# A hybrid attention and mixture-of-experts layer: weight buffers on 512-byte boundaries, one transpose in another PSUM pool, and four additions in another order

## The chip, the cores and the metric

The kernel runs on one core of a Trainium2 chip, in float32. The metric is the device time of one execution in microseconds, the median of three runs. A profile is one more execution of the same program, with every instruction and every DMA packet recorded.

## What is computed

One layer of an encoder on 256 tokens of width 1024. The first half is a token mixer: a projection (`w_in`), differential attention beside a gated linear recurrence, two branch projections and an output projection. The second half, where nearly all the time goes, is a mixture of 32 experts of which each token uses 4:

```python
logits = xf @ router_w + router_b
top_v, top_i = lax.top_k(logits, 4)
gates = softmax(top_v)
# for each expert e, on the tokens xb that chose it:
gu = xb @ w_gate_up[e] + b_gate_up[e]      # 1024 -> 2048
g, u = split(gu, 2); g = min(g, 7); u = clip(u, -7, 7)
y = ((u + 1) * g * sigmoid(1.702 * g)) @ w_down[e] + b_down[e]   # 1024 -> 1024
out[token] += gate * y
```

Each expert has 8 MB of gate and up weights and 4 MB of down weights; all 32 are read once, 384 MB in all.

## The kernel before, in words

**Weight pieces.** Weights go through buffers of 8 KB per partition and 1 MB in all, called pieces. Pieces 0 to 15 lie in the pool `arena`, on the left of SBUF right behind the pool `const`; pieces 16 to 18 lie in the pool `mo`, on the right (L71, L861 to L863). The pieces are used in turn, 19 of them during the experts (`chunk` and `spot`, L85 to L92; the DMA is issued on L87, on SyncE's queue). A gate-and-up piece holds 128 rows of 8 KB, one per partition; a down piece holds two rows of 4 KB per partition. A piece can be loaded again when the last matmul that reads it is done.

**Where they start.** The left side begins with 16,512 bytes that the language reserves. Then come the tiles of `const`, among them `x` (8192 bytes per partition), `r2` (8 bytes, which take a slot of 32, L176), `acc` (8192) and `bgu` (4096). In the program that is built the arena starts at byte 40,480, which is 79 times 512 plus 32; as every piece is 8192 bytes long, all 16 start 32 bytes past a multiple of 512. The pool `mo` hangs from the right end; its pieces start at byte 190,432 and every 8192 on, 480 past a multiple of 512 (224 past one of 256). Its last tile is `w2` (4096 bytes, L1139).

**An expert.** The loop from L1131 takes the experts in order. Tokens are gathered for two experts at a time into `xg` (`gather`, L907; two gathers of two banks' worth stand in most experts behind the gate and up products, L1179). An expert takes one of three shapes by its number of tokens: up to 32 (`gate_up_32`, L948, `down_32`, L975), up to 64 (`gate_up_64`, `down_64`), and above 64, where the tokens from the 65th to the 96th are a first, extra pass: L1155 to L1159 for the products into `po`, and L1188 to L1190 for the rest. Call these three-step experts the heavy ones. Each choice is a branch that TensorE, VectorE and ScalarE take, and TensorE's order over the branches is written out by hand (`step`, `in_turn`).

The second half of an expert is, on TensorE, in this order: `transposed` (L958: the activation is turned in two banks, T1 in `psb` copied by ScalarE and T2 in `psc` copied by VectorE), `turned` (L992: the combination weights `gd` or `gdo` are turned, copied by ScalarE to `gt`), the down products (L972 or L980), and `combine` (L997: products of `gt` and `y` into four banks, two of `psc` and two of `psb`, then four additions to `acc` on VectorE, L1007). In a heavy expert this is done twice, first for the extra tokens with `so` and `gdo`, then for the first 64 with `act` and `gd`.

**PSUM.** There are three pools: `psa` with 4 banks, `psb` with 2, `psc` with 2 (L58 to L60). Each call of `bank` takes the next bank of its pool and waits until its last reader is done. Before, an expert takes three banks of `psa` (`pg`, `pu`, `po`, L1148). From `psc` it takes the gathers' banks, T2, the one of `turned` (L1020, `bank(psc)` where `pt` is None) and the first two of `combine`; from `psb` T1, the down products' bank `py`, and the last two of `combine`. The last expert has `pt` and `other` in `psa` (L1185), since its additions are left out and sums stay in PSUM.

Of the kernel before, what the change touches and what calls it, by code (L numbers as in the profile page):

```python
# [12 lines left out]
F32 = mybir.dt.float32  # L13
# [9 lines left out]
P = 128  # L23
D = 1024
S = 256
KD = D // P
NT = S // P
# [11 lines left out]
U = 32  # L39
# [10 lines left out]
def kernel(ctx, tc, a, out):  # L50
    nc = tc.nc

    const = ctx.enter_context(tc.tile_pool(name="const", bufs=1, side="left"))
# [4 lines left out]
    psa = ctx.enter_context(tc.tile_pool(name="psa", bufs=4, space=PSUM))  # L58
    psb = ctx.enter_context(tc.tile_pool(name="psb", bufs=2, space=PSUM))
    psc = ctx.enter_context(tc.tile_pool(name="psc", bufs=2, space=PSUM))  # L60

    def bank(pool, *shape):
        t = pool.tile([P, 512], F32, name="bank")
        if not shape:
            return t
        if len(shape) == 2:
            return t[:, : shape[0] * shape[1]].rearrange("p (a b) -> p a b", b=shape[1])
        return t[:, : shape[0]]
# [16 lines left out]
    def chunk(src, *shape):  # L85
        v = part(spot(), 0, *shape)
        nc.sync.dma_start(v, src)  # L87
        return v
# [5 lines left out]
    def part(t, off, *shape):  # L94
        t = ar(t) if isinstance(t, int) else t
        v = t[:, off : off + int(np.prod(shape))]
        if len(shape) == 2:
            return v.rearrange("p (a b) -> p a b", b=shape[1])
        if len(shape) == 3:
            return v.rearrange("p (a b c) -> p a b c", b=shape[1], c=shape[2])  # L100
        return v
# [71 lines left out]
    nc.gpsimd.iota(iota, pattern=[[1, S + CA]], base=1, channel_multiplier=0, allow_small_or_imprecise_dtypes=True)  # L173

    xn2 = part(11, 0, NT, D)
    r2 = const.tile([P, NT], F32, name="r2")  # L176
    acc = const.tile([P, NT, D], F32, name="acc")
    gw2 = const.tile([P, KD], F32, name="gw2")
    s2 = late.tile([P, D], F32, name="s2")
# [40 lines left out]
    pt = bank(psb, KD)  # L220
# [95 lines left out]
    pt = bank(psb, P)  # L316
# [544 lines left out]
    mo = ctx.enter_context(tc.tile_pool(name="mo", bufs=2, side="right", reuse_waits="tile"))  # L861
# [130 lines left out]
    def turned(gd, gt, pt):  # L992
        for t in range(NT):
            nc.tensor.transpose(pt[:, t * P : (t + 1) * P], gd[:, t], ident)  # L994
        nc.scalar.copy(gt, pt[:, :S])  # L995

    def combine(gt, y, n):  # L997

        pcs = [bank((psc, psb)[c // 2], NT, 256) for c in range(4)]
        order = range(4) if n == U else (0, 2, 1, 3)  # L1000
        for t in range(NT):
            for c in order:
                r, w = (U * c, 0) if n == U else (C * (c // 2), 256 * (c % 2))
                nc.tensor.matmul(pcs[c][:, t], gt[r : r + n, t * P : (t + 1) * P], y[r : r + n, w : w + 256], start=True, stop=True)  # L1004
        for c in order:
            cs = slice(256 * c, 256 * (c + 1))
            nc.vector.tensor_tensor(acc[:, :, cs], acc[:, :, cs], pcs[c], ALU.add)  # L1007

    def combine_into(fin, gt, y, n):

        for t in range(NT):
            for c in (range(4) if n == U else (0, 2, 1, 3)):
                r, w = (U * c, 0) if n == U else (C * (c // 2), 256 * (c % 2))
                nc.tensor.matmul(fin[c][:, t], gt[r : r + n, t * P : (t + 1) * P], y[r : r + n, w : w + 256],  # L1014
                                 start=False, stop=True, skip_group_check=True)

    def out_of(at, wd, n, y, gd, gt, fin, pt):

        py = bank(psb)
        turned(gd, gt, bank(psc) if pt is None else pt)  # L1020
        (down_64 if n == C else down_32)(at, wd, py)
        w = 512 if n == C else 256
        nc.scalar.copy(y[:, :w], py[:, :w])  # L1023
        combine(gt, y, n) if fin is None else combine_into(fin, gt, y, n)
# [47 lines left out]
    def rare(spare):  # L1072

        engines = [ET.PE, ET.Activation, ET.DVE, ET.SP]
        of = lambda i: nc.values_load(counts[0:1, i : i + 1], engines=engines, min_val=0, max_val=S)
        xr = mo.tile([P, KD, EB * CA], F32, name="xg")
        with tc.If(of(NE) > CA) as some:
            for e in range(NE):
                cnt = of(e)
                with tc.If(cnt > CA):  # L1080
                    rest_of(e, CA, xr, spare)
                    with tc.If(cnt > CA + P):
                        rest_of(e, CA + P, xr, spare)
        return some
# [17 lines left out]
    def load(e):  # L1102

        engines = [ET.PE, ET.Activation, ET.DVE]
        ins, (cnt,) = nc.values_load_multi_w_load_instructions(counts[0:1, e : e + 1], engines=engines, min_val=0, max_val=S,
                                                               skip_runtime_bounds_check_because="a sum of 256 zeros and ones")
        for i in ins:
            tc.keep_in_program_order(i)
        return cnt
# [3 lines left out]
    def step(ins):  # L1113

        if turns:
            tc.add_manual_dep(ins, turns[-1].name, NOSYNC, reason="order")
        turns.append(ins)
# [9 lines left out]

    down_loads = lambda e: [chunk(rows(a["w_down"][e], 2 * P * i, 2), 2, D) for i in range(4)]
    after = load(0)
    fin = pt = other = None  # L1130
    for e in range(NE):  # L1131
        j = e % EB
        cnt = after
        wg = [chunk(rows(a["w_gate_up"][e], P * k, 1), 1, 2 * DFF) for k in range(KD)]
        if e == NE - 1:
            wd = down_loads(e)
            step(rare(list(slots)[: len(slots) - KD - 4]).cond_inst)
        if e == LASTS:
            w2 = mo.tile([P, D], F32, name="w2", bufs=1)  # L1139
            for n, pr in enumerate(rows_of(gw2, psc)):  # L1140
                nc.scalar.copy(w2[:, 512 * n : 512 * (n + 1)], pr)
        if j == 0:
            xgn, todo = gather_batch(e + EB) if e + EB < NE else (None, [])
            fill = first if e == 0 else todo[:2]
        elif e < NE - 1:
            fill = todo[0 if e == 1 else 2 :] + (down_bias() if e == LASTS else [])
        xe = xg[:, :, j * CA : (j + 1) * CA]
        pg, pu, po = bank(psa), bank(psa), bank(psa)  # L1148
        act = mo.tile([P, 512], F32, name="s", bufs=1)
        so = mo.tile([P, 256], F32, name="so", bufs=1)  # L1150
        gd = mo.tile([P, NT, P], F32, name="gd", bufs=1)
        gdo = mo.tile([P, NT, P], F32, name="gdo", bufs=1)
        for ks in (range(4), range(4, KD)):
            last = ks[-1] == KD - 1
            with tc.If(cnt > C) as more:  # L1155
                gate_up_32(e, po, xe, wg, ks, C)
                if last:
                    swiglu(po[:, :256], po[:, 256:], so)
                    weights(e, gdo, C, U)  # L1159
            step(more.cond_inst)  # L1160
            with tc.If(cnt > U) as many:
                gate_up_64(e, pg, pu, xe, wg, ks)
                if last:
                    swiglu(pg, pu, act)
                    weights(e, gd, 0, C)
            with many.Else():
                gate_up_32(e, pg, xe, wg, ks, 0)
                if last:
                    swiglu(pg[:, :256], pg[:, 256:], act[:, :256])
                    weights(e, gd, 0, U)  # L1170
            step(many.cond_inst)
        if e == NE - 1:
            fin = [bank(pool, NT, 256) for pool in (psc, psc, psa, psa)]

            def begin(c):
                return nc.tensor.matmul(fin[c], ident, acc[:, :, 256 * c : 256 * (c + 1)], start=True, stop=False, skip_group_check=True)

            fill = [lambda c=c: begin(c) for c in range(4)]
        for g in fill:  # L1179
            in_turn(g)  # L1180
        if e < NE - 1:
            after = in_turn(lambda: load(e + 1))
            wd = down_loads(e)
        else:
            pt, other = bank(psa), bank(psa)  # L1185
        at = mo.tile([P, 4, P], F32, name="actT", bufs=1)
        y, gt = mo.tile([P, 512], F32, name="y", bufs=1), mo.tile([P, S], F32, name="gt", bufs=1)
        with tc.If(cnt > C) as more:  # L1188
            transposed(so, at[:, 0:2], 2, other)
            out_of(at[:, 0:2], wd, U, y, gdo, gt, fin, pt)  # L1190
        step(more.cond_inst)
        with tc.If(cnt > U) as many:
            transposed(act, at, 4, other)
            out_of(at, wd, C, y, gd, gt, fin, pt)
        with many.Else():
            transposed(act[:, :256], at[:, 0:2], 2, other)
            out_of(at[:, 0:2], wd, U, y, gd, gt, fin, pt)
        step(many.cond_inst)
        if j == EB - 1:
            xg = xgn  # L1200
# [72 lines left out]
```

## Time and profile before

| | us |
|---|---|
| median of 3 runs | 1243.11 (1241.19 to 1246.12) |
| the profiled execution, its own time | 1242.41 |
| its span | 1240.4 |
| TensorE busy in the span | 1009.2 (81%) |
| VectorE busy | 430.8 (35%) |
| ScalarE busy | 227.7 (18%) |
| DMA, mean over the span | 375 GB/s, 465.70 MB |

The span runs from the first to the last recorded instruction; 2.0 us of the profiled execution lie around it. The token mixer takes the first quarter, and the experts' weights flow from there to about 20 us before the end. TensorE's busy time counts matmuls from start to modelled end, so that a busy engine is not one at its peak.

### The profile page before, as it was taken

The page shows a single profiled execution, that of the slowest core. Times are in us where ns is not written, and L with a number is a line of the kernel's source. Part 1 is how long each engine was busy: PE and PEld are TensorE (multiplying, and loading weights), DVE is VectorE, ACT ScalarE, POOL GpSimd, SP SyncE. Part 2 cuts the span into 40 slices and gives each one's busy share as a digit, 9 for nine tenths or more (in the row PEclk, how much of TensorE's full clock was granted, in tenths as well). Part 3 has the DMA queues.
Part 4 walks back from the last instruction along what each step waited for, and adds up shares of the span by engine and source line. Part 5 has one row for each costly group of instructions (what it writes and reads, how often), then busy time and mean ns, then how long its engine had stood idle before and what let it go on. Part 6 is the DMA issues. An engine that isn't in the chain of part 4 may idle for free. (4 is left out here: it accounts for less than half of the span.)

```text
span 1240.4 us, 17345 instructions
## 1 busy us (share of the span) xinstructions
PE 1009.2 (81%) x6774; PEld 520.6 (42%) x6774; DVE 430.8 (35%) x843; ACT 227.7 (18%) x426; POOL 26.6 (2%) x36
## 2 busy tenths in 40 slices
PE   6999999998779899888799789668776667787845
PEld 3767777864433333433344333223332222333312
DVE  3498779642222222322222232212222212121212
ACT  3544656331111000100001110000100000010001
POOL 1020100010000000000000000000000000000000
PEclk9999989989999999999999999889989887888978
DMA  9967669879999999799999999999999999999994
GB/s 343 337 242 280 204 215 352 320 319 397 411 413 415 413 415 414 316 391 388 415 413 414 414 413 413 413 415 416 414 413 413 415 412 414 407 407 408 413 411 180
DMA packets 100191, 465.70 MB, mean 375 GB/s; under 512 B 9716, under 2 KB 9814, under 8 KB 67256
## 3 DMA queue, kind: packets, MB, share of 16 engines
q1 hardware_dynamic: 100024, 463.31, 93.7%
q8 instruction: 125, 2.05, 0.7%
q14 instruction: 42, 0.34, 0.1%
HBM read 462.23 MB, written 1.05 MB: 373 GB/s over the span
## 5 line engine op out<-in xcount | busy, mean ns | idle before, releaser
L955 PE MATMUL bank<-piece,xg 128*32 128x512 f32 x1472 | 209.7, 684 | 66.7 <-DMA piece<-in_w_gate_up_dram 54.8
L945 PE MATMUL bank<-piece,xg 128*64 128x512 f32 x768 | 170.7, 596 | 3.6 <-PEq L1155 2.7
L1007 DVE TENSOR_TENSOR acc<-acc,bank 128x512 f32<-128x512 f32 x136 | 84.4, 682 | 249.2 <-PE bank L1004 249.2
L923 DVE TENSOR_SCALAR bank<-bank 128x256 f32<-128x256 f32 (+1 forms) x35 | 18.3, 524 | 373.4 <-PE bank L955 260.4
L955 PEld LDWEIGHTS bank<-piece,xg 128*32 128x32 f32 x1472 | 43.8, 117 | 207.7 <-DMA piece<-in_w_gate_up_dram 123.8
L980 PE MATMUL bank<-piece,actT 128*32 128x256 f32 x1472 | 99.3, 421 | 6.0 <-DMA piece<-in_w_down_dram 2.7
L924 ACT ACTIVATE s<-bank 128x256 f32<-128x256 f32 (+1 forms) x32 | 14.8, 463 | 480.0 <-DVE bank L923 480.0
L945 PEld LDWEIGHTS bank<-piece,xg 128*64 128x64 f32 x768 | 56.1, 138 | 111.5 <-issue 100.5
L913 PEld LDWEIGHTS bank<-oh,x 128*128 128x128 f32 x512 | 87.7, 203 | 31.7 <-issue 22.0
L913 PE MATMUL bank<-oh,x 128*128 128x192 f32 (+1 forms) x512 | 96.8, 346 | 0.4 <-DVE xg L905 0.4
L972 PE MATMUL bank<-piece,actT 128*64 128x512 f32 x384 | 86.5, 604 | 0.8
L130 PE MATMUL bank<-lo,piece 128*128 128x512 f32 x208 | 84.1, 404 | 3.3 <-DVE lo L122 3.3
L131 PE MATMUL bank<-hi,piece 128*128 128x512 f32 x208 | 83.9, 403 | 0.0
L129 PE MATMUL bank<-hi,piece 128*128 128x512 f32 x208 | 82.6, 402 | 0.0
L122 DVE TENSOR_TENSOR lo<-piece,hi 128x1024 fp32r<-128x1024 f32 x60 | 74.0, 1254 | 16.7 <-ACT hi L121 16.5
L980 PEld LDWEIGHTS bank<-piece,actT 128*32 128x32 f32 x1472 | 49.3, 120 | 50.7 <-issue 18.3
L121 ACT CAST hi<-piece 128x1024 fp32r<-128x1024 f32 x60 | 62.0, 1047 | 45.0 <-PE bank L131 36.7
L964 PE MATMUL bank<-ident,s 128*128 128x128 f32 x88 | 17.0, 299 | 63.1 <-DVEq L1188 29.1
L1004 PE MATMUL bank<-y,gt 32*128 32x256 f32 (+1 forms) x544 | 49.2, 396 | 21.0 <-ACT y L1023 21.0
L1004 PEld LDWEIGHTS bank<-y,gt 32*128 32x128 f32 (+1 forms) x544 | 33.4, 185 | 44.2 <-ACT y L1023 42.1
L972 PEld LDWEIGHTS bank<-piece,actT 128*64 128x64 f32 x384 | 26.8, 139 | 52.8 <-issue 48.0
L1023 ACT COPY y<-bank 128x256 f32<-128x256 f32 (+1 forms) x35 | 15.6, 445 | 179.4 <-PE bank L980 96.9
(265 smaller groups left out, 875.2 us busy)
## 6 DMA issues: line engine op xcount, KB each, us to landing
piece<-in_w_gate_up_dram SPq DMA_DIRECT2D x256, 1024.0 KB, 20.2
piece<-in_w_down_dram SPq DMA_DIRECT2D x128, 1024.0 KB, 20.3
piece<-in_w_in_dram SPq DMA_DIRECT2D x22, 1024.0 KB, 6.6
piece<-in_w_mod_dram SPq DMA_DIRECT2D x16, 1024.0 KB, 8.3
piece<-in_w_mod_dram SPq DMA_DIRECT2D x16, 512.0 KB, 7.0
piece<-in_w_out_dram SPq DMA_DIRECT2D x4, 1024.0 KB, 5.1
piece<-in_w_branch_a_dram SPq DMA_DIRECT2D x2, 1024.0 KB, 8.0
piece<-in_w_branch_b_dram SPq DMA_DIRECT2D x2, 1024.0 KB, 7.5
```

The costliest lines, as they stand in the source:

```text
L121: now(A, lambda: nc.scalar.copy(hi, v[:, h]))
L122: now(V, lambda: nc.vector.tensor_tensor(lo, v[:, h], hi.bitcast(F32), ALU.subtract))
L129: nc.tensor.matmul(out, ah, bh, start=start, stop=False, skip_group_check=True)
L130: nc.tensor.matmul(out, ah, bl, start=False, stop=False, skip_group_check=True)
L131: return nc.tensor.matmul(out, al, bh, start=False, stop=stop, skip_group_check=True)
L913: last = nc.tensor.matmul(ph[:, j], x[:, t, k * P : (k + 1) * P], oh[:, t, cs], start=t == 0, stop=t == NT - 1)
L945: nc.tensor.matmul(pp[r : r + C], xg[:, k, :C], wg[k][:, 0, 512 * q : 512 * (q + 1)], start=False, stop=k == KD - 1, skip_group_check=True)
L955: nc.tensor.matmul(halves(po[U * q : U * q + U]), xg[:, k, s0 : s0 + U], quarter(wg[k][:, 0], q), start=False, stop=k == KD - 1, skip_grou ...
L972: nc.tensor.matmul(py[C * n : C * n + C], at[:, j, C * half : C * half + C], wd[kk // 2][:, kk % 2, 512 * n : 512 * (n + 1)], start=kk == ...
L980: nc.tensor.matmul(py[U * c : U * c + U, 0:256], at[:, j, U * q : U * q + U], wd[kk // 2][:, kk % 2, 256 * c : 256 * (c + 1)], start=kk == ...
L1004: nc.tensor.matmul(pcs[c][:, t], gt[r : r + n, t * P : (t + 1) * P], y[r : r + n, w : w + 256], start=True, stop=True)
L1007: nc.vector.tensor_tensor(acc[:, :, cs], acc[:, :, cs], pcs[c], ALU.add)
```

## The change

`r2` is given 512 bytes per partition instead of 8 and cut back to its two columns; `w2` is given 480 bytes more. The slot of `r2` grows from 32 to 512 bytes, so everything behind it on the left moves up by 480 bytes: the arena then starts at 40,960, 80 times 512. The pool `mo` grows by 480 and hangs from the right, so its pieces move down by 480, to 189,952, 371 times 512. The other tiles of `mo` move with them.

The bank of `turned` is taken from `psa` for every expert, once ahead of the branches, and serves both passes of a heavy one. An expert thus takes four banks of `psa`, which has four, and one fewer per pass of `psc`.

In `combine`, the passes over 32 tokens or fewer take the four banks in the order 2, 0, 3, 1 instead of 0, 1, 2, 3, in the products and in the additions. Banks 0 and 1 are of `psc`, 2 and 3 of `psb`.

```diff
@@ -173,7 +173,7 @@
-    r2 = const.tile([P, NT], F32, name="r2")
+    r2 = const.tile([P, P], F32, name="r2")[:, :NT]
@@ -997,7 +997,7 @@  def combine(gt, y, n):
         pcs = [bank((psc, psb)[c // 2], NT, 256) for c in range(4)]
-        order = range(4) if n == U else (0, 2, 1, 3)
+        order = (2, 0, 3, 1) if n == U else (0, 2, 1, 3)
@@ -1017,7 +1017,7 @@  def out_of(at, wd, n, y, gd, gt, fin, pt):
-        turned(gd, gt, bank(psc) if pt is None else pt)
+        turned(gd, gt, pt)
@@ -1127,7 +1127,7 @@
-    fin = pt = other = None
+    fin = other = None
@@ -1136,7 +1136,7 @@
         if e == LASTS:
-            w2 = mo.tile([P, D], F32, name="w2", bufs=1)
+            w2 = mo.tile([P, D + 120], F32, name="w2", bufs=1)[:, :D]
@@ -1182,7 +1182,8 @@
         else:
-            pt, other = bank(psa), bank(psa)
+            other = bank(psa)
+        pt = bank(psa)
```

## Rows read from the trace of the kernel before

**Rows 1.** The page: 40 equal slices of the span, 31 us each.

```profile
DMA  9967669879999999799999999999999999999994
GB/s 343 337 242 280 204 215 352 320 319 397 411 413 415 413 415 414 316 391 388 415 413 414 414 413 413 413 415 416 414 413 413 415 412 414 407 407 408 413 411 180
```

**Rows 2.** Windows: length, busy PE, PEld, DVE, ACT, POOL, clock, DMA share, GB/s.

```profile
440.00:460.00 20.00, 19.01 (x109) 7.64 (x106) 6.05 (x13) 2.16 (x5) 0.00 (x0) 1.00 1.02 419
...
480.00:500.00 20.00, 20.00 (x130) 6.08 (x124) 4.73 (x12) 0.38 (x1) 0.00 (x0) 1.00 1.01 412
500.00:520.00 20.00, 16.17 (x140) 8.57 (x138) 7.70 (x16) 3.26 (x8) 0.00 (x0) 1.00 0.70 279
...
580.00:1040.00 460.00, 356.19 (x2610) 149.37 (x2610) 113.37 (x251) 41.66 (x98) 0.00 (x0) 0.92 1.02 414
```

**Rows 3.** Waits of PE, 300 to 1222 us: total us, times, longest.

```profile
PE bank L955 <- DMA piece<-in_w_gate_up_dram: 54.8, 51, 2.2
PE bank L964 <- DVEq L1188: 28.0, 20, 1.9
...
PE bank L994 <- DVE xg L905: 3.3, 3, 1.2
```

**Rows 4.** The view of rows 2, three windows of 2 us where the transfers stop.

```profile
514.00:516.00 2.00, 1.93 (x13) 0.84 (x12) 0.47 (x2) 0.74 (x2) 0.00 (x0) 1.00 0.04 8
516.00:518.00 2.00, 2.00 (x12) 0.57 (x8) 0.00 (x0) 0.00 (x0) 0.00 (x0) 1.00 0.22 49
518.00:520.00 2.00, 2.00 (x12) 0.72 (x10) 0.00 (x0) 0.00 (x0) 0.00 (x0) 1.00 0.93 365
```

**Rows 5.** PE's timeline in two heavy experts: start, length, instructions, idle time before.

```profile
458.55 0.38 PE L964 MATMUL bank<-ident,so 128*128 128x128 f32 x2
459.92 0.41 PE L994 MATMUL bank<-ident,gdo 128*128 128x128 f32 x2 [0.99 <-DVE xg L905]
460.26 3.66 PE L980 MATMUL bank<-piece,actT 128*32 128x256 f32 x64
...
467.66 0.63 PE L964 MATMUL bank<-ident,s 128*128 128x128 f32 x4 [2.05 <-DVE acc L1007]
468.12 0.56 PE L994 MATMUL bank<-ident,gd 128*128 128x128 f32 x2
468.61 3.83 PE L972 MATMUL bank<-piece,actT 128*64 128x512 f32 x10
...
513.60 0.63 PE L964 MATMUL bank<-ident,s 128*128 128x128 f32 x4 [2.05 <-DVE acc L1007]
...
514.52 7.09 PE L972 MATMUL bank<-piece,actT 128*64 128x512 f32 x32
```

**Rows 6.** DVE's and ACT's timelines in the first of them, same columns.

```profile
459.29 0.48 DVE L905 TENSOR_SCALAR xg<-bank,sa,modc 128x192 f32<-128x192 f32 x1 [0.82 <-ACT xg L904]
459.69 0.28 DVE L965 COPY actT<-bank 128x128 f32<-128x128 f32 x1
465.63 2.48 DVE L1007 TENSOR_TENSOR acc<-acc,bank 128x512 f32<-128x512 f32 x4 [5.66 <-PE bank L1004]
468.32 0.42 DVE L965 COPY actT<-bank 128x256 f32<-128x256 f32 x1 [0.21 <-PE bank L964]
...
459.16 0.26 ACT L965 COPY actT<-bank 128x128 f32<-128x128 f32 x1
```

**Rows 7.** L994, all its matmuls on `gdo`: ns min/median/max, first and last start.

```profile
L994 PE MATMUL bank<-ident,gdo x6: 272/286/301, 459.9 to 861.3; 128*128 128x128 f32 x6
```

**Rows 8.** Windows as in rows 2: three `mo` pieces land; then sixteen `arena` pieces.

```profile
602.75:610.26 7.51, 6.25 (x36) 2.61 (x32) 0.92 (x2) 0.58 (x1) 0.00 (x0) 1.00 1.03 421
...
748.21:755.75 7.54, 7.22 (x36) 2.37 (x34) 0.03 (x1) 0.00 (x0) 0.00 (x0) 1.00 1.01 406
...
610.26:651.26 41.00, 33.50 (x243) 14.04 (x244) 10.93 (x25) 3.01 (x7) 0.00 (x0) 0.96 1.02 414
...
997.53:1038.45 40.92, 30.17 (x200) 12.19 (x196) 9.67 (x23) 3.81 (x9) 0.00 (x0) 0.75 1.02 413
```

## The prediction

> **What bounds the kernel now.** I read the slices first [rows 1]: from the ninth on the DMA engines are busy throughout and move 407 to 416 GB/s, except in slices 17 to 19 (316, 391, 388) and the last. The 384 MB of the experts, not an arithmetic engine, therefore set three quarters of the time: windows over the long undisturbed stretch give 414 GB/s at a DMA share of 1.02 [rows 2]. (The share passes 1 because the packets' recorded times overlap a little.) PE's waits say the same from the other side: it waits 54.8 us for gate and up pieces [rows 3]. So a change is worth something here in three ways only: if the transfers run faster, if they stop less often, or if the tail after the last piece is shorter.
>
> The transfers stop once for long, in the window of 500 to 520 us, which moves 279 GB/s instead of 414 [rows 2]: (1 - 279/414) x 20 = 6.5 us lost. The 2 us windows show the bottom at 514 to 518 us and the stream back at 518 [rows 4]. PE's timeline says why [rows 5]. Two heavy experts follow each other there, and between them PE is the late one: it is busy for all of the 20 us from 480 to 500 [rows 2]. The queue ran dry because the down pieces of the second heavy expert were still to be read; the first of them came free some matmuls into L972, which starts at 514.52, and the transfers came back 2 to 3 us later. There, and nowhere else in the experts, PE's chain is the path.
>
> **The change, part by part.** 1. *The bank of `turned`.* In the first pass of a heavy expert L994 waits for VectorE's gather (L905), because `turned` gets the `psc` bank that the second gather still holds: 0.99 us in the first heavy expert [rows 5], 3.3 us in three [rows 3]. With a bank of `psa` it can follow T2 at 458.55 + 0.38 = 458.93. But what comes next is late as well. L980 takes its first four matmuls from ScalarE's copy, ready at 459.16 + 0.26 = 459.42, and the others from VectorE's copy behind the same gather, ready at 459.69 + 0.28 = 459.97 [rows 6]. At 3.66/64 = 0.057 us each, 60 of them from 460.0 end at 463.45, against 460.26 + 3.66 = 463.92: 0.5 us are won, not 0.99. In the second heavy expert VectorE's copy is later in its queue, and I count 0.2. On the other experts' path there is nothing to win: L994 waits nowhere else, T1 and T2 before it do.
>
> 2. *The order of the additions.* T1 of the second pass waits 2.05 us [rows 5], since its `psb` bank is the one of the third addition; the four take 2.48 us from 465.63, 0.62 each [rows 6]. In the new order that bank is read first, so T1 can start at 465.63 + 0.62 + 0.15 = 466.4 instead of 467.66. Where T2 stands depends on part 1: with one `psc` bank fewer per pass its bank is that of the second addition, free at 467.0. Then `turned` (0.23 after T2's start, as the same four transposes take 0.46 now) and L972 at 467.8 instead of 468.6: 0.8 us. What is late next is VectorE's copy of T2, which stands behind all four additions in its queue and ends at 468.11 + 0.42 = 468.5. It is needed from L972's fifth matmul on, and four take 4 x 7.09/32 = 0.9 us, to 468.7: just covered. The new product order costs nothing by itself: the same 16 instructions with the same shapes in other banks. In light experts the next user of those banks comes behind all of the next expert's gate and up products, and nothing changes.
>
> So a heavy expert gains 0.8 + 0.2 to 0.5, about 1.1 us. Three are heavy, as L994 turns `gdo` six times, two transposes each, the last at 861 us [rows 7]. The first two both lie ahead of the stop, on PE's path, and bring the free pieces 2.2 us earlier; the third is covered by a full queue, whose stretch runs at 414 GB/s [rows 2]. The far ends: nothing, if the transfers that come back meet another late piece; 6.5 us, the whole stop.
>
> 3. *Four banks of `psa` out of four.* The next expert's `pg` no longer finds a bank that rested for a whole expert, but the one of this expert's `pg`. Its last readers are VectorE's steps of the activation, which come ahead of T1 of the same expert; the first product comes after `combine`. I take 0, with up to 2.48 us per expert (VectorE's additions, [rows 6]) as the far end on the slow side. No step is moved past a DMA queue or past POOL: the changes touch PE, ACT and DVE only, and SP's order is the same.
>
> 4. *The boundaries.* No piece of the kernel before starts on a multiple of 512, but the two kinds start differently: 32 bytes past one of 256 in the arena, 224 past one in `mo`. So the trace can say what the distance costs. Counted in bytes back from the end of the stream, three `mo` pieces land in a row every 19 MB. The nine such windows between 600 and 1000 us average 414.2 GB/s (406 to 421), and the nine of arena pieces behind them 413.9 (413 to 416) [rows 8]. The difference, 0.3, is within what nine windows with a scatter of 5 can say, 1.6 GB/s or 0.4%. I take 0. The rows cannot test a distance of zero. The far end for a gain is the best 20 us window, 419 GB/s [rows 2]: 937 us of stream (285 to 1222) x (1 - 414/419) = 11 us. For a loss it is the 0.4%, 4 us.
>
> The rows on the landing pieces are what speaks here. [...]
>
> The sum: against the profiled execution 1242.41 - 2.2 = 1240.2; that execution is 0.7 below the median, so the forecast is 1243.1 - 2.2 = 1240.9. A measurement of this kernel can tell about 0.5%, 6.2 us, from no change; the forecast lies within that.
>
> **Rivals.** *The boundaries pay.* Then the stream runs as in its best window, 1240.9 - 11 = 1230. For it: no row excludes a gain at distance zero, and the stream's rate sets the time. Against it: two kinds of distance, one rate [rows 8]. I give it 0.16. [...]
>
> *The spare bank is missed* (slower). The first product of an expert waits until VectorE is through its additions. For it: PE does wait 28.0 us in 20 places for VectorE to reach a branch [rows 3], although the banks concerned were long free, so a wait on an old reader can be put down to a later point. Then PE loses up to 31 x 2.48 = 77 us. 55 of them fall in time that it waits for weights anyway [rows 3], so that it decides from about 55/31 = 1.8 us per expert on; at the full price 1240.9 + 22 = 1263. Against it: the second product bank, `pu`, already follows `pg` of the expert before, and no wait of L945 for VectorE shows. 0.07.
>
> *VectorE takes it back.* The copies of T1 and T2 gate the down products, and the second heavy pass gains nothing because its copy stands behind the additions: then 1243. This is also the time if the order of banks comes out otherwise than I counted. 0.10.
>
> **How the numbers follow.** The forecast's own case has 0.67, with 1237 to 1245: the sum, less or plus the 4 us of part 4. Faster by over 0.5% (below 1236.9): most of the 0.16 and a little of the main case's edge, 0.17. Slower by over 0.5% (above 1249.3): 0.07. Within: 0.76. The range reaches to 1233 on the side of the boundaries, into that rival but not to its end, and to 1247 on the other, the loss of 4 us and the spread of runs; it leaves out the missed bank and the far part of the boundaries' gain.
>
> **What would show it.** Right: L994's wait for L905 gone; T1 of the second heavy pass waiting about 0.8 us instead of 2.05, L972 following within 1.5 us; the stop at 514 to 518 us shorter by about 2 us; the long stretch still at 414 GB/s. Wrong: 416 GB/s or more over 580 to 1040 us (the boundaries pay), or a wait of L935, L945 or L955 for VectorE at the start of an expert (the missed bank).

## The result, and the profile after

The changed kernel takes 1228.59 us (median of 4 runs, 1223.81 to 1229.64) against 1242.15 before: a ratio of 0.988, 95% interval [0.9842, 0.9917]. (A ratio and its interval are estimated from all runs of both kernels; it can differ by up to 0.2% from the ratio of the two medians.) The forecast was 1240.9 with a range from 1233 to 1247, so the time lies outside, on the fast side. What happened is the first rival: the boundaries pay. The profiled execution took 1229.55 us with a span of 1227.6.

The slices of the page after (40 slices, 30.7 us each) show it at a glance beside [rows 1]:

```profile
GB/s 348 359 234 274 202 188 349 310 330 369 415 421 423 422 423 423 317 399 379 424 421 423 422 422 422 422 423 423 424 422 420 423 421 420 417 413 421 422 413 174
```

Over the long stretch (slices 20 to 34), where 412 to 416 stood, 420 to 424 stands. The stop is still in slices 17 to 19. The windows of [rows 2] and [rows 4] for the kernel after (length, busy time of the engines, clock, DMA share, GB/s):

```profile
440.00:460.00 20.00, 20.00 (x113) 7.60 (x110) 4.95 (x11) 1.49 (x3) 0.00 (x0) 1.00 1.02 426
...
500.00:520.00 20.00, 17.76 (x140) 8.87 (x138) 7.30 (x16) 3.17 (x8) 0.00 (x0) 0.91 0.69 273
...
580.00:1040.00 460.00, 363.39 (x2718) 153.04 (x2718) 116.49 (x257) 42.54 (x100) 0.00 (x0) 0.92 1.02 422
...
514.00:516.00 2.00, 2.00 (x10) 0.74 (x8) 0.00 (x0) 0.00 (x0) 0.00 (x0) 0.74 0.00 0
516.00:518.00 2.00, 2.00 (x12) 0.62 (x10) 0.00 (x0) 0.00 (x0) 0.00 (x0) 1.00 0.65 172
```

The long stretch runs at 422 GB/s instead of 414, 1.9% more, at the same DMA share. The stop costs about as much as before (273 instead of 279 GB/s in its window).

The heavy experts on PE's timeline (start, length, instructions, idle time before), to be read beside [rows 5]:

```profile
460.50 0.38 PE L964 MATMUL bank<-ident,so 128*128 128x128 f32 x2
460.72 0.38 PE L994 MATMUL bank<-ident,gdo 128*128 128x128 f32 x2
461.43 3.78 PE L980 MATMUL bank<-piece,actT 128*32 128x256 f32 x64 [0.32 <-ACT actT L965]
465.76 1.15 PE L1004 MATMUL bank<-y,gt 32*128 32x256 f32 x16 [0.55 <-ACT y L1023]
467.75 0.41 PE L964 MATMUL bank<-ident,s 128*128 128x128 f32 x2 [0.85 <-DVE acc L1007]
468.35 0.41 PE L964 MATMUL bank<-ident,s 128*128 128x128 f32 x2 [0.19 <-DVE acc L1007]
468.60 0.38 PE L994 MATMUL bank<-ident,gd 128*128 128x128 f32 x2
468.91 7.09 PE L972 MATMUL bank<-piece,actT 128*64 128x512 f32 x32
...
512.24 8.45 PE L972 MATMUL bank<-piece,actT 128*64 128x512 f32 x32
...
557.54 0.62 PE L935 MATMUL bank<-bgu,sel 96*32 96x512 bf16 x4 [4.06 <-issue]
```

This part came as forecast: L994 follows T1 and T2 at once, T1 of the second pass waits 0.85 us instead of 2.05, T2 0.19 more, and L972 follows. From L964 on `so` to L972 the first heavy expert takes 468.91 - 460.50 = 8.41 us; before, 468.61 - 458.55 = 10.06 [rows 5].

Where the 14 us come from is read from two instructions that both kernels issue in the same order: the first product of the expert behind the stop (L935), and the first of the last sums (L1176). Before:

```profile
558.60 0.62 PE L935 MATMUL bank<-bgu,sel 96*32 96x512 bf16 x4 [4.14 <-issue]
...
1218.14 3.70 PE L1176 MATMUL bank<-acc,ident 128*128 128x512 f32 x8
```

After:

```profile
1204.01 3.70 PE L1176 MATMUL bank<-acc,ident 128*128 128x512 f32 x8
```

At L935 the kernel after is 1.1 us ahead (557.54), at L1176 14.1 us. Between them lie 660 us of stream, and 660 x (1 - 414/422) = 12.5 us is what the rate explains of the 13.1. Ahead of the stop the faster stream won nothing that lasts; the experiments come back to this.

### The profile page after: what moved, and what is told of

Read it like the earlier page. It is cut to its first block, busy times and chain, and to the rows that moved or that the text cites. A ratio compares the mean times of both kernels' runs of the same rounds, so it can differ in the third digit from the quotient of the medians.

```text
span 1227.6 us, 17342 instructions
## 1 busy us (share of the span) xinstructions
PE 1010.9 (82%) x6774; PEld 521.1 (42%) x6774; DVE 429.9 (35%) x843; ACT 227.6 (19%) x426; POOL 25.5 (2%) x36
## 3 DMA queue, kind: packets, MB, share of 16 engines
q8 instruction: 125, 2.05, 0.6%
## 5 line engine op out<-in xcount | busy, mean ns | idle before, releaser
L955 PE MATMUL bank<-piece,xg 128*32 128x512 f32 x1472 | 209.6, 688 | 58.3 <-DMA piece<-in_w_gate_up_dram 45.7
L945 PE MATMUL bank<-piece,xg 128*64 128x512 f32 x768 | 170.4, 594 | 4.8 <-PEq L1155 2.7
L955 PEld LDWEIGHTS bank<-piece,xg 128*32 128x32 f32 x1472 | 45.1, 118 | 201.9 <-DMA piece<-in_w_gate_up_dram 106.9
L945 PEld LDWEIGHTS bank<-piece,xg 128*64 128x64 f32 x768 | 55.5, 137 | 112.6 <-issue 100.6
L972 PE MATMUL bank<-piece,actT 128*64 128x512 f32 x384 | 86.4, 603 | 0.7
L964 PE MATMUL bank<-ident,s 128*128 128x128 f32 x88 | 17.2, 295 | 55.8 <-DVEq L1189 34.8
L972 PEld LDWEIGHTS bank<-piece,actT 128*64 128x64 f32 x384 | 26.9, 139 | 52.4 <-issue 49.1
```

The costliest lines, as they stand in the source:

```text
L945: nc.tensor.matmul(pp[r : r + C], xg[:, k, :C], wg[k][:, 0, 512 * q : 512 * (q + 1)], start=False, stop=k == KD - 1, skip_group_check=True)
L955: nc.tensor.matmul(halves(po[U * q : U * q + U]), xg[:, k, s0 : s0 + U], quarter(wg[k][:, 0], q), start=False, stop=k == KD - 1, skip_grou ...
L972: nc.tensor.matmul(py[C * n : C * n + C], at[:, j, C * half : C * half + C], wd[kk // 2][:, kk % 2, 512 * n : 512 * (n + 1)], start=kk == ...
```

## The experiments

The kernels ran in four groups, each beside the kernel before; its median in the four was 1243.67, 1245.02, 1244.95 and 1245.34 us. All ratios are to it.

**The two halves of the change.** The paddings alone, on the kernel before:

```diff
-    r2 = const.tile([P, NT], F32, name="r2")
+    r2 = const.tile([P, P], F32, name="r2")[:, :NT]
-            w2 = mo.tile([P, D], F32, name="w2", bufs=1)
+            w2 = mo.tile([P, D + 120], F32, name="w2", bufs=1)[:, :D]
```

> The two paddings alone; banks and order of the additions as before. Theory 1 (the boundaries made the stream faster): the long stretch runs at 422 GB/s as after the whole change, the two heavy experts keep their waits of 2.05 us, and the time is about 2 us above the changed kernel: 1230 to 1231 us, ratio about 0.990. Theory 2 (the shorter heavy experts made the gain and the rate follows from fewer stops): 414 GB/s and about 1240 to 1242 us.

Measured: 1232.26 us, ratio 0.9887 [0.9857, 0.9917], and the long stretch:

```profile
580.00:1040.00 460.00, 364.37 (x2722) 155.02 (x2714) 114.00 (x251) 42.87 (x101) 0.00 (x0) 0.91 1.02 422
```

The other half, the kernel after without the paddings (the diff above, undone):

> The bank of the combination weights and the order of the additions alone; pieces at 32 and 480 past a multiple of 512 as before. Theory 1: 414 GB/s in the long stretch, the waits in the heavy experts as in the changed kernel, and about 2 us less than before: 1240 us, ratio 0.998. Theory 2: 422 GB/s and about 1229 us, ratio 0.989.

Measured: 1239.63 us, ratio 0.9965 [0.9941, 0.9989].

```profile
580.00:1040.00 460.00, 359.47 (x2668) 152.02 (x2664) 111.12 (x246) 42.47 (x100) 0.00 (x0) 0.91 1.02 414
```

The rate goes with the paddings, whatever the heavy experts do: theory 2 falls. By the medians the paddings are worth 11.4 us and the banks with the order 4.0; by the intervals of the ratios, 10 to 18 us and 1.4 to 7.3. (The paddings move other tiles as well, `acc` among them; a run below, with half of the pieces off the boundary, moves pieces and the small tiles behind them alone, and the rate follows.)

**Which boundary.** The kernel after with other paddings, so that all 19 pieces start 64, 128 or 256 bytes past a multiple of 512 (the tile of `r2` has 16, 32 or 64 columns, and 120 of `w2` becomes 104, 88 or 56):

```diff
-    r2 = const.tile([P, P], F32, name="r2")[:, :NT]
+    r2 = const.tile([P, 64], F32, name="r2")[:, :NT]
-            w2 = mo.tile([P, D + 120], F32, name="w2", bufs=1)[:, :D]
+            w2 = mo.tile([P, D + 56], F32, name="w2", bufs=1)[:, :D]
```

> The changed kernel with all pieces 64 bytes past a multiple of 512. If a distance that is a multiple of 64 is enough, the stream runs at 422 GB/s and the time is that of the changed kernel, 1228 us. If it takes 256 or 512, the stream stays at 414 GB/s and the time is that of the banks alone, 1240 us; a value between would say that the cost grows with the distance.

Measured: 1236.5 us, ratio 0.9934 [0.9911, 0.9957].

```profile
580.00:1040.00 460.00, 360.52 (x2688) 152.30 (x2684) 113.34 (x249) 42.53 (x100) 0.00 (x0) 0.91 1.02 415
```

> The changed kernel with all pieces 128 bytes past a multiple of 512. At 256 the long stretch ran at 422 GB/s, at 64 at 415. Theory 1 (a transfer must start at a multiple of 256): 414 to 415 GB/s and 1236 to 1240 us. Rival (128 is enough): 422 GB/s and 1225 to 1229 us.

Measured: 1238.01 us, ratio 0.9943 [0.9919, 0.9966].

```profile
580.00:1040.00 460.00, 362.13 (x2672) 152.21 (x2668) 113.05 (x250) 42.45 (x100) 0.00 (x0) 0.91 1.02 415
```

> The changed kernel with all pieces 256 bytes past a multiple of 512. [...]

Measured: 1224.6 us, ratio 0.9837 [0.9805, 0.9869].

```profile
580.00:1040.00 460.00, 361.79 (x2716) 152.50 (x2716) 113.91 (x251) 42.47 (x100) 0.00 (x0) 0.93 1.02 422
```

At 256 the stream has its full 422 GB/s, at 128 and 64 it has 415, hardly more than at 32. Whether 256 is even better than 512, as 1224.6 against 1228.59 could suggest, was asked by the changed kernel once more:

> The changed kernel once more, beside the others: 1228 us by its four runs. With all pieces at 256 the time was 1224.6 us at the same 422 GB/s; if 512 and 256 are the same to the transfers, this run lies within 1224 to 1230 and its rate is 422.

Measured: 1224.53 us (1223.04 to 1229.51, 5 runs), ratio 0.9857 [0.983, 0.9884], 422 GB/s. So 256 and 512 are the same within the noise: the changed kernel's own medians differ by 4 us from one group of runs to the next.

**Does each piece pay for itself?** One padding without the other puts 3 or 16 of the 19 pieces off the boundary.

> The changed kernel with the padding of r2 alone: sixteen pieces on multiples of 512, the three on the right at 480 past one. If every piece pays for its own start, the long stretch runs at (16 x 422 + 3 x 414)/19 = 420.7 GB/s, the windows in which the three right pieces land at 414 and the others at 422, and the time is 1.9 us above the changed kernel's (3/19 of 11.8). If pieces that start off a boundary slow their neighbours in the queue too, the rate is nearer 414 and the windows don't differ.

Measured: 1227.1 us, ratio 0.9871 [0.9844, 0.9898].

```profile
580.00:1040.00 460.00, 360.67 (x2702) 150.12 (x2706) 113.85 (x251) 42.53 (x100) 0.00 (x0) 0.91 1.02 422
```

When each kind of piece passes can be counted: the 384 pieces of the experts stand in the order in which the program issues them, and their bytes are counted back from the end of the stream. By this count the windows of [rows 8] stand four pieces too late. The three `mo` pieces that the row 748.21:755.75 is said to hold pass at 737.0 to 744.5 us; and where they pass at 640.0 to 647.7, the last has landed by 650.1, before the window that was taken for them (651.26) begins. Placed by the count, over nine rounds, the three pieces at 480 land at 421.8 GB/s on average and the sixteen on the boundary at 421.3; in the changed kernel, with all on it, the same places have 421.6 and 422.4. Both theories fell: the three pieces don't pay the full price, nor do they slow the others.

> The changed kernel with the padding of w2 alone: the three pieces on the right on multiples of 512, the sixteen on the left at 32 past one. If every piece pays for its own start: 415.3 GB/s, the windows of the right pieces at 422, and 1237 to 1239 us. If one kind sets the pace of all: 422 or 414 in both kinds of window.

Measured: 1236.6 us, ratio 0.9933 [0.9899, 0.9968].

```profile
580.00:1040.00 460.00, 355.09 (x2684) 149.88 (x2680) 113.93 (x251) 42.46 (x100) 0.00 (x0) 0.93 1.02 416
```

Here the three pieces on the boundary land at 417.4 GB/s and the sixteen off it at 415.1, where paying for itself meant 422 and 414. In the kernel before the same places have 413.7 and 413.8. Windows of 7.5 us scatter by 5 GB/s and more, so the 417.4 is a rough figure.

With half of the pieces off the boundary, by 32 bytes more behind the eighth piece of the arena:

```diff
-    piece = lambda i, dt=F32: (arena if i < NA else mo).tile([P, 2048], dt, name="piece", tag=f"ar{i}", bufs=1)
+    piece = lambda i, dt=F32: (arena if i < NA else mo).tile([P, 2056 if i == 15 else 2048], dt, name="piece", tag=f"ar{i}", bufs=1)[:, :2048]
```

> The changed kernel with 8 of the 19 pieces 32 bytes past a multiple of 512 and 11 on one. With 19, 16, 3 and 0 pieces off the boundary the long stretch ran at 414, 416, 422 and 422 GB/s. If the loss goes as the share of pieces off the boundary, it is 8 x 8/19 = 3.4 and the rate 418.6. If it goes as the chance that two transfers off the boundary meet, the square of the share, it is 8 x 0.18 = 1.4 and the rate 420.6.

Measured: 1226.61 us, ratio 0.9854 [0.9816, 0.9892].

```profile
580.00:1040.00 460.00, 357.09 (x2696) 149.81 (x2692) 113.75 (x251) 42.54 (x100) 0.00 (x0) 0.93 1.02 420
```

| pieces off the boundary | measured, GB/s | if the loss goes as their share | as the square of it |
|---|---|---|---|
| 19 of 19 | 414 | 414 | 414 |
| 16 of 19 | 416 | 415.3 | 416.3 |
| 8 of 19 | 420 | 418.6 | 420.6 |
| 3 of 19 | 422 | 420.7 | 421.8 |
| 0 of 19 | 422 | 422 | 422 |

Neither law fits all three rates between the ends. With one more digit, from the packets' sizes and starts, these are 415.5, 419.7 and 421.7: the share is too low by 0.2, 1.1 and 1.0, the square too high by 0.8, 0.9 and 0.1. The five kernels with all pieces on the boundary and all experts' work lie within 0.3 of each other, so the loss does not add up piece by piece. The same padding of `w2` is worth 1.7 GB/s beside sixteen pieces off the boundary (413.8 to 415.5) and 0.3 beside sixteen on it (421.7 to 422.0).

In the run with half of them, six pieces off the boundary and then six on it stand in a row in each round. One round, and the same places in the changed kernel:

```profile
885.06:900.47 15.41, 13.75 (x155) 5.62 (x154) 3.81 (x8) 1.02 (x4) 0.00 (x0) 1.00 1.01 412
900.47:915.42 14.95, 10.34 (x98) 6.12 (x96) 3.39 (x10) 2.40 (x6) 0.00 (x0) 0.77 1.01 423
...
889.87:905.09 15.22, 13.62 (x152) 4.92 (x150) 3.37 (x7) 1.01 (x3) 0.00 (x0) 1.00 1.02 418
905.09:919.96 14.87, 10.56 (x96) 6.50 (x96) 3.82 (x11) 2.42 (x6) 0.00 (x0) 0.77 1.02 425
```

Over eleven rounds the six off the boundary land at 415.3 GB/s and the six on it at 421.5; in the changed kernel the same places have 420.3 and 421.7. So six in a row do pay, 5 GB/s of the 8. The packets' own durations say it with less scatter. A packet of 8 KB takes 313 ns (median) in the kernel before and 309 in the changed one. With half of the pieces off, it takes 313 in the middle of the six off the boundary and 309 in the middle of the six on it. But in the middle of three pieces it takes 309 both when they alone are on the boundary and when they alone are off it. So the price is not the transfer's own alone; it depends on what else passes around it. Six in a row at 32 bytes past paid and three at 480 did not; whether the number in a row or the distance makes that difference was not tried apart.

**Where the gain ahead of the stop went.** The kernel after without the extra pass of the heavy experts (their tokens from the 65th to the 96th are left out), with the pieces on and off the boundary; the condition is changed in both places where it stands:

```diff
-        with tc.If(cnt > C) as more:
+        with tc.If(cnt > S - 1) as more:
```

> The changed kernel without the extra pass of the three heavy experts (their tokens from the 65th to the 96th are left out). If the stop at 514 us gives back what the faster stream wins ahead of it, then without the stop the boundaries are worth the rate's difference over the whole stream, 937 x (1 - 414/422) = 17.8 us, between this kernel and the same one with the pieces off the boundary. If the gain ahead of 514 us is lost elsewhere, the difference stays at 11 to 14 us.

> The same kernel without the extra pass, with the banks and the order of the change, but the pieces at 32 and 480 past a multiple of 512 as before. Both theories: 414 GB/s. With the stop as the cause: 17 to 18 us above the kernel with the pieces on the boundary; otherwise 11 to 14.

Measured: 1216.2 us (0.9766 [0.9731, 0.9801]) on the boundary and 1235.65 (0.9912 [0.9884, 0.9941]) off it. The slices of the page, first on, then off:

```profile
GB/s 352 357 234 286 208 203 363 310 321 383 417 421 423 422 423 422 422 422 423 422 422 423 421 422 422 421 417 422 421 420 417 422 416 422 408 417 416 418 420 157
```

```profile
GB/s 340 341 242 284 193 197 345 320 324 391 400 413 414 414 414 414 414 414 415 413 414 415 414 414 413 413 408 416 408 415 408 413 410 408 408 404 412 411 409 169
```

The stop is gone in both, and the boundaries are now worth 19.5 us by the medians, a little more than the 17.8 expected, and not 11 to 14. Off the boundary the long stretch ran at 412 GB/s, not at the 414 expected, and on it at 420.

The intervals of these two times are wide, about 4 us either way each, but the profiles agree. From the first L994, at the start of the experts, to the first L1176 the two take 899.8 and 917.2 us, 17.4 apart. With the extra pass it is 909.2 and 907.9 on the boundary (the changed kernel's two profiles) and 921.0 off it (banks and order alone), 12 to 13 apart. And from the first L994 to L935 behind the stop these three take 262.7, 263.2 and 262.0 us: with the stop, nothing of the gain is left there. The reading is that PE sets when the transfers come back at 517 us, whatever the stream's rate was till then. The stop therefore takes back what the stream wins in its first 230 us.

**Bank and order apart.** The bank alone, on the kernel before (`order` as it was, the paddings undone):

> The bank of the combination weights in the products' pool alone; order of the additions and boundaries as before. L994's wait for the gather is gone and L980 waits for VectorE's copy in its place, 0.2 to 0.5 us won in a heavy expert; T1 of the second pass keeps its wait of 2.05 us. 1241 to 1243 us, and 414 GB/s. If instead the bank is the larger part of the 4 us that both won, about 1240.

Measured: 1245.37 us, ratio 1.0009 [0.9988, 1.003]. PE's timeline in the first heavy expert:

```profile
459.25 0.38 PE L994 MATMUL bank<-ident,gdo 128*128 128x128 f32 x2
459.95 3.78 PE L980 MATMUL bank<-piece,actT 128*32 128x256 f32 x64 [0.32 <-ACT actT L965]
...
467.47 1.09 PE L964 MATMUL bank<-ident,s 128*128 128x128 f32 x4 [2.04 <-DVE acc L1007]
...
468.92 9.43 PE L972 MATMUL bank<-piece,actT 128*64 128x512 f32 x32
```

The order alone, on the kernel before:

```diff
-        order = range(4) if n == U else (0, 2, 1, 3)
+        order = (2, 0, 3, 1) if n == U else (0, 2, 1, 3)
```

> The order of the additions alone; bank and boundaries as before. Theory 1 (the order does all that bank and order did together, as the wait of 2.04 us that it shortens also costs the clock of the products behind it): T1 of the second pass waits about 0.85 us, L972 in the first heavy expert takes 7.1 us at a granted clock of 1.00 instead of 8.6 at 0.91, and the time is that of both, 1240 us, ratio 0.9965. Rival (the two need each other, since the bank of T2 comes free only with the other pool): T2 waits longer, and 1242 to 1243 us.

Measured: 1243.84 us, ratio 0.9992 [0.9971, 1.0013].

```profile
473.73 0.41 PE L964 MATMUL bank<-ident,s 128*128 128x128 f32 x2 [0.85 <-DVE acc L1007]
474.32 0.41 PE L964 MATMUL bank<-ident,s 128*128 128x128 f32 x2 [0.19 <-DVE acc L1007]
475.52 0.66 PE L994 MATMUL bank<-ident,gd 128*128 128x128 f32 x2 [0.79 <-DVE acc L1007]
```

The waits bear the rival out: the two need each other. (The times agree, but 0.9965 for both, 1.0009 and 0.9992 for one alone, lie within each other's noise when added up.) With the order alone T1 comes early, and then `turned` waits 0.79 us, as its `psc` bank is that of the fourth addition: 0.85 + 0.19 + 0.79 = 1.83 us in place of 2.05. With the bank alone T1 keeps its wait. Only where `turned` has left `psc` does the early T1 reach L972. The last run says the same in the changed kernel:

> The changed kernel without the bank: both paddings and the order of the additions. If the bank of the combination weights is worth nothing, the time is that of the changed kernel, 1224 to 1229 us, and the long stretch runs at 422 GB/s. If it is worth 0.2 to 0.5 us in each heavy expert ahead of the stop, up to 1 us more than that.

Measured: 1230.62 us, ratio 0.9885 [0.9851, 0.992], the same as the paddings alone (0.9887), with the wait of 0.79 us back in each heavy expert. No version that was tried and computes the whole layer beats the changed kernel by more than the noise.

## Why the prediction was wrong

What bounds the kernel was read rightly: the stream sets the time behind the stop, PE ahead of it, and "if the transfers run faster" was the first of the three ways named.

The step that failed is part 4, "I take 0". It compared pieces 32 bytes past a boundary with pieces 224 past one, found 414 GB/s for both, and took the lack of a difference for the lack of a cost. All pieces were off a boundary, so the comparison had no case without the cost. Starts at 32 (with three pieces at 480), 64 and 128 bytes past a multiple of 512 give 414 to 415 GB/s, starts at 256 and 0 give 422: the term put at 0 is 8 GB/s, 2% of the rate, and 11.4 us. The sentence that the rows can't test a distance of zero stood in the text, yet the 4 us on either side, which became the main case's range, were taken from that comparison. They priced the scatter of a contrast that did not contain the case to be forecast.

The comparison was also misplaced: by the count above, its `mo` windows hold pieces of the arena. Placed right, it gives 413.7 and 413.8 GB/s, the same null. Even in the right place such short windows tell little: with the three `mo` pieces on the boundary and the sixteen others off it, they read 417.4 against 415.1. What 480 costs when all pieces are there, no run shows.

That the far end of 11 us met the 11.4 of the paddings is luck: the stream rose to 422 and not to 419, and the gain came from the 660 us behind the stop and not from 937. A gain at distance zero, which no row excluded, deserved the middle of the range, not 0.16.

Twice the distance did not cost more: 64 and 128 bytes past a multiple of 512 both give 415 GB/s. Why 256 is enough and 128 is not, no run shows.

Part 1 was right as a bound: what comes next is late as well, and the bank alone is worth nothing that could be measured. Part 2 was right in its waits (0.8 forecast, 0.85 measured) and in that T2's bank depends on part 1; that `turned` itself would wait for the fourth addition if it stayed in `psc` was not seen. The term may have been too small: 2.2 us forecast, 4.0 measured for bank and order together, with an interval of 1.4 to 7.3. In the first heavy expert 10.06 - 8.41 = 1.65 us were won instead of 1.1, and L972 behind it shows a further part, 7.09 us instead of 8.55. That instruction and the stretch of 460 to 480 us, before:

```profile
468.61 8.55 PE L972 MATMUL bank<-piece,actT 128*64 128x512 f32 x32
...
460.00:480.00 20.00, 16.66 (x140) 7.60 (x144) 3.40 (x6) 2.07 (x5) 0.00 (x0) 0.91 1.02 414
```

and with bank and order but without the paddings:

```profile
460.00:480.00 20.00, 17.67 (x162) 7.53 (x154) 5.81 (x11) 1.70 (x4) 0.00 (x0) 1.00 1.02 412
```

The granted clock is 0.91 there before, with 0.60, 0.50, 0.50 and 0.70 in the four microseconds from 468 on and 1.00 in the others, and 1.00 over the whole stretch with the shorter wait. All three runs that keep the wait of 2.04 us have it at 0.83 to 0.91 in the stretch of the first heavy expert. But in the second one the kernel before has the same wait and then 7.09 us for L972 [rows 5]; with 1.83 us in three parts it was 0.87 with the order alone and 1.00 with the paddings beside it, and the changed kernel fell to 0.91 in its second heavy expert (8.45 us above). That the wait causes the fall is thus argued and not shown.

The missed spare bank did not come: the waits of L935, L945 and L955 for VectorE that it would show are absent from the changed kernel, and the kernel with the bank alone is at 1.0009.

## What to carry to other kernels

Where a stream of weights sets the time, as here, let every buffer that it fills start at a multiple of 256 bytes (starts at 0 and 256 bytes past a multiple of 512 gave 422 GB/s here, at 64 and 128 past 415), and work the starts out from the tile sizes: here one tile of 8 bytes had moved sixteen buffers off it, and with the three others the stream ran at 414 GB/s, 2% less. A comparison inside one trace tests only the values that the trace contains; where the new value is not among them, a null result there bounds nothing. Windows that are said to hold certain transfers should be placed by a count that the landings confirm. And a wait that a bank causes can move to the next user of the pool when only one of the two is changed, as the 2.05 us did here (0.79 of it went to `turned`); look for the second before pricing the first.

## What the runs showed that was not expected

The loss is not additive. With 16 of 19 buffers on the boundary the stream already runs at 422 GB/s, and with 8 off it at 420, while all 19 off it cost 8. Six buffers in a row at 32 bytes past paid (415.3 GB/s against 420.3 in the changed kernel), three at 480 did not (421.8 against 421.6). Why is open; what besides the starts could matter was not tried apart, nor was a kernel with all buffers at 480.

The first stage ends at different times from one profile to the next. The first L994, at the start of the experts, falls between 289.0 and 295.7 us over the sixteen profiles, on the boundary (289.0 and 294.8 for the changed kernel's two) as well as off it. That is half a per cent of the time: of the 6.6 us between the changed kernel's two profiled spans, 5.8 stand there already. It is likely much of the 3 to 4 us between medians of one kernel, too.
